# GpSimd work moved away from the routing chain, and unsplit 32-column conditioning products, in a hybrid attention and expert block

## The chip, the cores and the metric

One core of one Trainium2 chip. The metric is the device time of one execution in microseconds (us); less is better. The core has a tensor engine (PE, with its weight loads listed apart as PEld), a vector engine (DVE), a scalar engine (ACT), GpSimd (POOL), and a sync engine (SP) that here only issues transfers. Sixteen DMA engines carry all transfers.

## The reference

One layer over 512 latent tokens and 256 context tokens of width 1024. Six modulation vectors come from `silu(c) @ w_ada + b_ada` (w_ada is 1024 x 6144), for the latent vector c and for the context vector c_ctx. The tokens are normalized and modulated, projected by one matrix, and go through two attentions (grouped-query, and differential with 4 heads), which are gated, merged and projected; the result is added to x. Then comes the expert layer:

```
logits = h @ router_w + router_b;  top 4 of 32 experts per token, softmax over the 4
gate = min(xe @ w_gate[e] + b_gate[e], 7);  up = clip(xe @ w_up[e] + b_up[e], -7, 7)
act = (up + 1) * (gate * sigmoid(1.702 * gate));  y = act @ w_down[e] + b_down[e]
x = x + g_m * (sum of the token's 4 expert outputs, weighted)
```

All is float32. The 32 experts' matrices are 32 x 3 x 4 MB and are read once.

## The kernel before, in words

**Precision.** A float32 product is either made directly (the tensor engine then runs each product as two instructions, each with its own weight load), or "split": ACT rounds the weight block to fp32r (`wh`), DVE or POOL subtracts to get the rest (`wl`), and two or three faster fp32r products replace the one.

**Conditioning** (lines 181 to 314). The first two modulation vectors (`w_ada` columns 0 to 2047, two halves `hf` of 8 row blocks `k` of 512 KB each) are needed before anything can be projected. SP loads the blocks in order; even blocks go to four buffers `araw`, odd ones to two buffers `wraw` and a third spare one. After the second block SP loads the four tiles of x (512 KB each) and, after block 5, two small tables (256 KB each). Blocks 1 and 4 of a half are multiplied directly (two products of 128x512), the other six are split on ACT (L163) and DVE (L164) and take four fp32r products each. The left operand has only 4 columns (c and c_ctx, high and low parts), so the result stands in 4 partitions of `p_mod`. `columns` (L258) copies each 512-wide row out of PSUM, turns it into columns with four small transposes, and adds the bias (L267, L268); L313 finishes the scale `Ac`. Between the products the tensor engine transposes the normalized x (`channels`, 8 times 4 transposes, L227). After that the projections start.

**The middle** (lines 419 to 916) is projections, attention and their merge. The last three modulation vectors but one are summed on DVE as `acc` and `gm_bc` and spread over the partitions by `ada_end` (L679: two direct products with ones of 128x512, two ACT copies); `gm_bc` (the gate of the expert layer) is finished at L892, although it is first read by the experts.

**Output projection and routing** (lines 919 to 1104). Eight groups of products (n = 0, 1 by token tile i = 0 to 3) make x1 = x + attention. For n = 1 each tile then goes through a chain: `scaled` (L1004, two halves on POOL), `routed` (an rsqrt on DVE, L1013 makes h2, L1014 and L1015 write h2 and x1 to DRAM from POOL's queue, the last h2 from ACT's), and three stages that run later: transposes, logits (16 instructions on the tensor engine, then a string of small 128x32 operations on DVE, L1028 to L1043, that finds the top 4) and ranks (L1045). The stages of the last tiles are issued under `tc.high_priority(300)` (L1171). Then expert 0 is placed (`placed`, `gathered`: one-hot, positions, an indirect gather of its tokens from POOL's queue), the counts of all experts are sorted (L1219 to L1258), which ends in `perm` (L1246), the order in which the other 31 experts are taken. SP reads `perm` to know which weights to load next.

**The experts** (lines 1108 to 1424). Weights come in blocks of 1 MB (384 of them) into 13 places, which become free as blocks are used up. The first 12 blocks belong to expert 0 and are loaded while the routing runs; block 13 and later need `perm`. Experts alternate: a large one (128 slots, its weights split; `ahead` runs the ACT cast L1158 and the subtraction L1160 up to four half blocks in front of the tensor engine) and a small one (64 slots, direct products in two groups of 64 columns, L1284, whose places the products themselves free). The first four subtractions are on POOL, all later ones on DVE. `ahead(3)` (L1216) makes the first three half blocks ready before the sort. The two zeroed buffers `xg` for gathered tokens are set at L1167. The loop at L1408 stands under `tc.manual_schedule`: on PE, ACT and DVE its order is the written one, with small jobs hooked in ahead of a product's block k. One of them is `act_of(l + 1)`, four transposes of the small expert's activations at block 4 of the large expert's `down`.

Elsewhere a scheduler orders each engine's instructions by readiness and priority, and each engine and each transfer queue then works strictly in that order.

Of the kernel before, what the change touches and what calls it, by code (L numbers as in the profile page):

```python
# [32 lines left out]
def tile_hybrid_block(  # L33
# [169 lines left out]
    sil4 = sp.tile([128, NK, 4], FT, name="sil4")  # L203
    DVE.memset(sil4, 0.0)
    silr = sp.tile([128, NK, 4], FR, name="silr")
    for w in range(2):
        DVE.tensor_copy(sil4[:, :, 2 * w], sil[:, :, w])
        DVE.tensor_copy(silr[:, :, 2 * w], sil[:, :, w])
        DVE.tensor_sub(silr[:, :, 2 * w + 1], sil[:, :, w], silr[:, :, 2 * w])
# [45 lines left out]
    p_mc = ps.tile([128, 16, 4], FT, name="pc", bufs=1)  # L255
    md = sp.tile([128, 16, 2], FT, name="md")

    def columns(hf):  # L258

        for n in (2 * hf, 2 * hf + 1):  # L260
            row = xin[0:4, n % 2, 0:512] if hf else hraw[6 + n][0:4]
            (ACT.copy if n % 2 else DVE.tensor_copy)(row, p_mod[0:4, n])
            for j in range(4 * n, 4 * n + 4):
                PE.transpose(p_mc[:, j], row[:, (j % 4) * 128:(j % 4 + 1) * 128], ident[:4, :4])
        js = slice(8 * hf, 8 * hf + 8)
        pairs = p_mc[:, js].rearrange("p j (w a) -> p j w a", a=2)
        DVE.tensor_add(md[:, js], pairs[:, :, :, 0], col(cols[:, 24 + 8 * hf:32 + 8 * hf], 2))  # L267
        DVE.tensor_add(md[:, js], md[:, js], pairs[:, :, :, 1])  # L268

    for hf in range(2):  # L270
        for k in range(NK):
            w = w_ada[k * 128:(k + 1) * 128, hf * D:(hf + 1) * D].rearrange("p (o d) -> p o d", o=1)
            if k in (0,2,4,6):
                raw = sp.tile([128, 1, D], FT, name="araw", bufs=4)
                SP.dma_start(raw, w)
            else:
                raw = load_raw(w, 1, D)
            if k in (1,4):
                for n in range(2):
                    mm(p_mod[0:4, 2 * hf + n], sil4[:, k], raw[:, 0, n * 512:(n + 1) * 512], False, k == NK - 1)  # L280
            else:
                h, l = split_w(raw)
                for n in range(2):
                    ns = slice(n * 512, (n + 1) * 512)
                    mm(p_mod[0:4, 2 * hf + n], silr[:, k], h[:, 0, ns], k == 0, False)
                    mm(p_mod[0:4, 2 * hf + n], silr[:, k], l[:, 0, ns], False, k == NK - 1)
# [605 lines left out]
    for a, scale in ((acc[0], 0.5), (acc[1], 1.0), (gm_bc, 1.0)):  # L892
        ada_end(ps.tile([128, D], FT, name="S", bufs=2), a, scale)
# [72 lines left out]

    def expert_bias(j):
# [32 lines left out]
    def scaled(i, n):  # L1000
# [3 lines left out]
        POOL.tensor_mul(h2s[i][:, ns], x1[i][:, ns], sc_bc[:, ns])  # L1004
# [65 lines left out]
    for n in range(2):  # L1070
        ns = slice(n * 512, (n + 1) * 512)
        for i in range(4):
            p = ps.tile([128, D], FT, name=("pg", "pu")[i % 2], bufs=1)[:, ns]
            if n:
                channels_x1(i, 0)
            for k in range(NK):
# [16 lines left out]
            if n:  # L1093
                scaled(i, 0)
# [56 lines left out]
    def ahead(n=BEFORE):  # L1151

        while len(split) < n and at_split[0] < len(to_split):
# [6 lines left out]
            (DVE if at_split[0] > 3 else POOL).tensor_sub(wl, raws[i][:, a], wh)  # L1160
# [5 lines left out]
    place, xg = {}, []  # L1166
    for b, n in enumerate((D, 512)):  # L1167
        t = xp.tile([128, n], FT, name=f"xg{b}")
        POOL.memset(t, 0.0)
        xg.append(t)  # L1170
# [41 lines left out]

    placed(0, one_hot(0))
    gathered(0)
    fetch(2)
    ahead(3)  # L1216
# [36 lines left out]
    DVE.tensor_copy(rkms, srt[:, 768:896].rearrange("p (i e) -> p i e", i=4))  # L1253
    weights = srt[:, 896:1024].rearrange("p (i e) -> p i e", i=4)
    DVE.tensor_copy(auxs[:, :, :, 1], weights)
    DVE.tensor_sub(auxs[:, :, :, 2], weights, auxs[:, :, :, 1])
    for u in range(2):
        POOL.tensor_add(halvesr[:, u], blocks[:, 2 * u], blocks[:, 2 * u + 1])  # L1258
    f1.close()
# [148 lines left out]
    with tc.manual_schedule(engines={mybir.EngineType.PE, mybir.EngineType.Activation, mybir.EngineType.DVE}):  # L1408
# [7 lines left out]
        for l in range(2, E, 2):  # L1416
# [4 lines left out]
            down(l, {1: lambda: input_of(l + 2), 4: lambda: act_of(l + 1)})  # L1421
# [129 lines left out]
```

## Time and profile before

| what | value |
|---|---|
| runs shown | 1625.44, 1627.09, 1629.03 us; median 1627.09 |
| the profiled execution | 1623.81 us, span of its instructions 1621.9 us |
| PE, PEld busy | 1537.2 us (95%), 1047.6 us (65%) |
| DVE, ACT, POOL busy | 1056.4 us (65%), 754.1 us (46%), 222.0 us (14%) |
| transfers | 483.43 MB, mean 298 GB/s |

The profile shows one execution. Each engine runs its own queue; a row of the timeline gives start, duration, engine, line, operation and operands, and in brackets how long the engine stood idle before it and what released it. A stall inside an instruction is no idle time: it appears as an instruction that is far longer than others of its kind. A matmul that follows another closely is listed longer than its share, since they overlap.

### The profile page before, as it was taken

To read this page: it belongs to the slowest core of one execution; us is meant where nothing else is said; L and a number is where in the kernel's file an instruction comes from. 1 tells how busy PE (TensorE), PEld (TensorE's weight loads), DVE (VectorE), ACT (ScalarE), POOL (GpSimd) and SP (SyncE) were. 2 spreads that over 40 slices of the span, in tenths; PEclk is the share of its full clock that TensorE was granted. 3 is DMA by queue.
4 is the path that set the end of the run, shared out by engine and by line. 5 is a ranking of instruction groups with operands and counts; after the bars stand their busy time and mean duration, and the time that the engine had idled before them with its cause. 6 is when DMAs were issued, how large, how long until landed. Compare 5 with 4: busy or idle time off the path is not lost. (4 is left out here: it accounts for less than half of the span.)

```text
span 1621.9 us, 20787 instructions
## 1 busy us (share of the span) xinstructions
PE 1537.2 (95%) x7303; PEld 1047.6 (65%) x7303; DVE 1056.4 (65%) x1668; ACT 754.1 (46%) x1051; POOL 222.0 (14%) x209
## 2 busy tenths in 40 slices
PE   7999999989999689999999999999999999999997
PEld 2778877778877564666666665656666565566564
DVE  6888888756877865566566575564565655656654
ACT  5668834256633243354445344443444434434442
POOL 3431000141001520010110110100101101001000
PEclk9999999999999879999999999999999999999999
DMA  8320055411365578999999999999999999999994
GB/s 315 91 66 27 27 169 166 146 53 40 105 194 208 220 290 356 405 403 421 406 405 423 402 410 408 394 413 395 398 412 387 411 402 387 418 389 395 411 401 153
DMA packets 102430, 483.43 MB, mean 298 GB/s; under 512 B 11393, under 2 KB 33082, under 8 KB 53170
## 3 DMA queue, kind: packets, MB, share of 16 engines
q1 hardware_dynamic: 91458, 453.71, 70.8%
q0 software_dynamic: 10720, 27.82, 6.0%
q8 instruction: 60, 0.98, 0.2%
q10 hardware_dynamic: 144, 0.52, 0.1%
q14 instruction: 48, 0.39, 0.1%
HBM read 473.62 MB, written 16.78 MB: 302 GB/s over the span
## 5 line engine op out<-in xcount | busy, mean ns | idle before, releaser
L1160 DVE TENSOR_TENSOR wl<-g,wh 128x1024 fp32r<-128x1024 f32 x110 | 130.7, 1222 | 61.0 <-ACT wh L1158 52.1
L1158 ACT CAST wh<-g 128x1024 fp32r<-128x1024 f32 x110 | 110.5, 1047 | 73.9 <-DMA g<-in_w_down_dram 31.9
L1160 DVE TENSOR_TENSOR wl<-raw,wh 128x1024 fp32r<-128x1024 f32 x86 | 103.9, 1239 | 53.4 <-ACT wh L1158 46.3
L1158 ACT CAST wh<-raw 128x1024 fp32r<-128x1024 f32 x90 | 90.9, 1047 | 62.8 <-DMA raw<-in_w_down_dram 23.8
L1160 DVE TENSOR_TENSOR wl<-x,wh 128x1024 fp32r<-128x1024 f32 x70 | 83.8, 1223 | 50.3 <-ACT wh L1158 42.0
L1158 ACT CAST wh<-x 128x1024 fp32r<-128x1024 f32 x70 | 71.2, 1048 | 70.0 <-DMA x<-in_w_down_dram 34.6
L1333 POOL CAST spread<-halvesr 128x128 fp32r<-128x128 f32 x16 | 4.6, 291 | 598.2 <-PE py L60 598.2
L60 PE MATMUL pg<-wh,xH 128*128 128x512 f32 x256 | 82.3, 403 | 0.0
L60 PE MATMUL pu<-wh,xH 128*128 128x512 f32 x256 | 81.8, 401 | 0.0
L60 PE MATMUL pg<-wh,xL 128*128 128x512 f32 x256 | 80.9, 397 | 0.0
L60 PE MATMUL pg<-wl,xH 128*128 128x512 f32 x256 | 80.6, 396 | 0.0
L60 PE MATMUL pu<-wh,xL 128*128 128x512 f32 x256 | 80.5, 395 | 0.0
L60 PE MATMUL pu<-wl,xH 128*128 128x512 f32 x256 | 80.5, 395 | 0.0
L564 DVE TENSOR_REDUCE mx<-S 128x1 f32<-128x768 f32 x64 | 60.4, 953 | 30.0 <-PE S L60 29.8
L567 ACT ACTIVATE P<-S,nb,rsq 128x768 f32<-128x768 f32 x64 | 63.6, 996 | 31.5 <-DVE nb L566 31.4
L1284 PE MATMUL py<-g,xS 128*64 128x512 f32 x328 | 77.6, 598 | 0.0
L163 ACT CAST wh<-wraw 128x1024 fp32r<-128x1024 f32 x54 | 56.8, 1055 | 40.7 <-DMA wraw<-in_w_in_dram 11.4
L1160 DVE TENSOR_TENSOR wl<-acc,wh 128x1024 fp32r<-128x1024 f32 x36 | 43.2, 1223 | 28.4 <-ACT wh L1158 23.9
L1160 DVE TENSOR_TENSOR wl<-y,wh 128x1024 fp32r<-128x1024 f32 x38 | 45.4, 1222 | 21.7 <-ACT wh L1158 18.1
L164 DVE TENSOR_TENSOR wl<-wraw,wh 128x1024 fp32r<-128x1024 f32 x39 | 47.9, 1232 | 16.9 <-ACT wh L163 16.8
L1284 PE MATMUL py<-raw,xS 128*64 128x512 f32 x248 | 58.7, 597 | 0.0
L60 PEld LDWEIGHTS pg<-wl,xH 128*128 128x128 f32 x256 | 48.3, 189 | 11.8
(466 smaller groups left out, 3734.4 us busy)
## 6 DMA issues: line engine op xcount, KB each, us to landing
g<-in_w_up_dram SPq DMA_DIRECT2D x42, 1024.0 KB, 18.6
g<-in_w_down_dram SPq DMA_DIRECT2D x38, 1024.0 KB, 19.7
g<-in_w_gate_dram SPq DMA_DIRECT2D x36, 1024.0 KB, 21.2
raw<-in_w_gate_dram SPq DMA_DIRECT2D x34, 1024.0 KB, 22.7
raw<-in_w_down_dram SPq DMA_DIRECT2D x29, 1024.0 KB, 17.7
raw<-in_w_up_dram SPq DMA_DIRECT2D x27, 1024.0 KB, 21.4
wraw<-in_w_ada_dram SPq DMA_DIRECT2D x40, 512.0 KB, 4.6
x<-in_w_gate_dram SPq DMA_DIRECT2D x20, 1024.0 KB, 23.5
```

What stands on the lines that cost most here:

```text
L60: PE.matmul(o, l, r, start=start, stop=stop)
L163: ACT.copy(h, raw)
L164: (sub or DVE).tensor_sub(l, raw, h)
L564: DVE.reduce_max(mx, S, axis=AX)
L567: ACT.activation(P, S, AF.Exp, bias=nb, scale=rs, accum_out=sm)
L1158: ACT.copy(wh, raws[i][:, a])
L1160: (DVE if at_split[0] > 3 else POOL).tensor_sub(wl, raws[i][:, a], wh)
L1284: PE.matmul(p[64 * n:64 * n + 64], X[:, k], raws[i][:, a, n * 512:(n + 1) * 512], start=False, stop=True, skip_group_check=True)
L1333: POOL.tensor_copy(s[:, :, 1], halvesr[:, :, r:r + 1].to_broadcast([128, 2, SLOTS]))
```

## The change

In the conditioning no block is split: the left operand is padded to 32 columns (`sil32`), block b writes to partitions 32 (b mod 4) onward, two blocks are taken at a time, and `fold` sums the four groups while it turns rows into columns. In the routing, the split subtractions, half of the last tile's `scaled` and the zeroing of `xg` are taken from POOL or done earlier, the first `ahead(3)` moves behind the sort, and `ada_end` of `gm_bc` moves to just ahead of the placing of expert 0. In the expert loop one hook moves from block 4 to block 5.

```diff
--- before.py
+++ after.py
@@ -200,13 +200,12 @@
     DVE.tensor_scalar(s2, s2, 0.5, 0.5, op0=OP.mult, op1=OP.add)
     DVE.tensor_mul(s2, s2, cc)
 
-    sil4 = sp.tile([128, NK, 4], FT, name="sil4")
-    DVE.memset(sil4, 0.0)
-    silr = sp.tile([128, NK, 4], FR, name="silr")
-    for w in range(2):
-        DVE.tensor_copy(sil4[:, :, 2 * w], sil[:, :, w])
-        DVE.tensor_copy(silr[:, :, 2 * w], sil[:, :, w])
-        DVE.tensor_sub(silr[:, :, 2 * w + 1], sil[:, :, w], silr[:, :, 2 * w])
+    sil32 = sp.tile([128, NK, 32], FT, name="sil32")
+    DVE.memset(sil32, 0.0)
+    DVE.tensor_copy(sil32[:, :, 0:2], sil)
+
+    fold = sp.tile([128, 2], FT, name="fold")
+    DVE.reduce_sum(fold, ident.rearrange("p (j m) -> p m j", m=32)[:, 0:2], axis=AX)
 
     ms = sp.tile([128, 8], FT, name="ms")
     rr = sp.tile([128, 8], FT, name="rr")
@@ -252,38 +251,36 @@
                 POOL.tensor_mul(o2[:, :, :, a], s4[:, :, :, a], rep(g2[:, :, 1 - a], 4))
 
     p_mod = ps.tile([128, 4, 512], FT, name="pmod")
-    p_mc = ps.tile([128, 16, 4], FT, name="pc", bufs=1)
+    p_mc = ps.tile([128, 16, 2], FT, name="pc", bufs=1)
     md = sp.tile([128, 16, 2], FT, name="md")
 
     def columns(hf):
 
         for n in (2 * hf, 2 * hf + 1):
-            row = xin[0:4, n % 2, 0:512] if hf else hraw[6 + n][0:4]
-            (ACT.copy if n % 2 else DVE.tensor_copy)(row, p_mod[0:4, n])
+            row = xin[:, n % 2, 0:512] if hf else hraw[6 + n]
+            (ACT.copy if n % 2 else DVE.tensor_copy)(row, p_mod[:, n])
             for j in range(4 * n, 4 * n + 4):
-                PE.transpose(p_mc[:, j], row[:, (j % 4) * 128:(j % 4 + 1) * 128], ident[:4, :4])
+                mm(p_mc[:, j], row[:, (j % 4) * 128:(j % 4 + 1) * 128], fold, True, True)
         js = slice(8 * hf, 8 * hf + 8)
-        pairs = p_mc[:, js].rearrange("p j (w a) -> p j w a", a=2)
-        DVE.tensor_add(md[:, js], pairs[:, :, :, 0], col(cols[:, 24 + 8 * hf:32 + 8 * hf], 2))
-        DVE.tensor_add(md[:, js], md[:, js], pairs[:, :, :, 1])
+        DVE.tensor_add(md[:, js], p_mc[:, js], col(cols[:, 24 + 8 * hf:32 + 8 * hf], 2))
 
     for hf in range(2):
+        raws = []
         for k in range(NK):
             w = w_ada[k * 128:(k + 1) * 128, hf * D:(hf + 1) * D].rearrange("p (o d) -> p o d", o=1)
-            if k in (0,2,4,6):
+            if k % 2 == 0:
                 raw = sp.tile([128, 1, D], FT, name="araw", bufs=4)
                 SP.dma_start(raw, w)
             else:
                 raw = load_raw(w, 1, D)
-            if k in (1,4):
+            raws.append(raw)
+            if k % 2:
+
                 for n in range(2):
-                    mm(p_mod[0:4, 2 * hf + n], sil4[:, k], raw[:, 0, n * 512:(n + 1) * 512], False, k == NK - 1)
-            else:
-                h, l = split_w(raw)
-                for n in range(2):
-                    ns = slice(n * 512, (n + 1) * 512)
-                    mm(p_mod[0:4, 2 * hf + n], silr[:, k], h[:, 0, ns], k == 0, False)
-                    mm(p_mod[0:4, 2 * hf + n], silr[:, k], l[:, 0, ns], False, k == NK - 1)
+                    for b in (k - 1, k):
+                        rows_ = slice(32 * (b % 4), 32 * (b % 4) + 32)
+                        PE.matmul(p_mod[rows_, 2 * hf + n], sil32[:, b], raws[b][:, 0, n * 512:(n + 1) * 512],
+                                  start=b < 4, stop=b >= 4, skip_group_check=True)
             if hf == 0 and k == 1:
                 for i in range(4):
                     SP.dma_start(xin[:, i], x2[i * 128:(i + 1) * 128])
@@ -889,7 +886,7 @@
             next(fill, None)
     opened["yp"] = open_pool("yp2", "right", stack=yst)
     yBH, yBL = halves("yB", yB, DVE)
-    for a, scale in ((acc[0], 0.5), (acc[1], 1.0), (gm_bc, 1.0)):
+    for a, scale in ((acc[0], 0.5), (acc[1], 1.0)):
         ada_end(ps.tile([128, D], FT, name="S", bufs=2), a, scale)
 
 
@@ -964,6 +961,12 @@
     for g in range(4):
         DVE.tensor_copy(diag[32 * g:32 * g + 32], marks[32 * g:32 * g + 32, 0, 32 * g:32 * g + 32])
 
+    xg = []
+    for b, n in enumerate((D, 512)):
+        t = rp.tile([128, n], FT, name=f"xg{b}")
+        POOL.memset(t, 0.0)
+        xg.append(t)
+
     def expert_bias(j):
         b = braw[32 * j:32 * j + 32]
         if j == 1:
@@ -1001,7 +1004,7 @@
         if n == 0:
             h2s[i] = fp.tile([128, D], FT, name="h2", bufs=2)
         ns = slice(n * 512, (n + 1) * 512)
-        POOL.tensor_mul(h2s[i][:, ns], x1[i][:, ns], sc_bc[:, ns])
+        (DVE if i == 3 and n else POOL).tensor_mul(h2s[i][:, ns], x1[i][:, ns], sc_bc[:, ns])
 
     def routed(i):
 
@@ -1073,6 +1076,7 @@
             p = ps.tile([128, D], FT, name=("pg", "pu")[i % 2], bufs=1)[:, ns]
             if n:
                 channels_x1(i, 0)
+                scaled(i, 0)
             for k in range(NK):
                 if n and i and k == 4:
                     stages[i - 1][0]()
@@ -1091,7 +1095,6 @@
             DVE.tensor_add(x1[i][:, ns], x1[i][:, ns], t)
             ACT.activation(t, x1[i][:, ns], AF.Square, scale=1.0 / 32.0, accum_out=sqs[:, i, n:n + 1])
             if n:
-                scaled(i, 0)
                 scaled(i, 1)
                 stages.append(routed(i))
                 if i:
@@ -1157,17 +1160,13 @@
             wh = xp.tile([128, D], FR, name="wh", bufs=BEFORE + 1)
             ACT.copy(wh, raws[i][:, a])
             wl = xp.tile([128, D], FR, name="wl", bufs=BEFORE)
-            (DVE if at_split[0] > 3 else POOL).tensor_sub(wl, raws[i][:, a], wh)
+            DVE.tensor_sub(wl, raws[i][:, a], wh)
             split[i, a] = wh, wl
             at_split[0] += 1
             if a:
                 used_up(i)
 
-    place, xg = {}, []
-    for b, n in enumerate((D, 512)):
-        t = xp.tile([128, n], FT, name=f"xg{b}")
-        POOL.memset(t, 0.0)
-        xg.append(t)
+    place = {}
     with tc.high_priority(300):
         stages[3][0]()
         stages[2][2]()
@@ -1210,10 +1209,10 @@
             in_offset=bass.IndirectOffsetOnAxis(ap=place[e][0][:, 0:1], axis=0),
             bounds_check=(2 * T if small else T) - 1, oob_is_err=False)
 
+    ada_end(ps.tile([128, D], FT, name="pg", bufs=1), gm_bc, 1.0)
     placed(0, one_hot(0))
     gathered(0)
     fetch(2)
-    ahead(3)
 
 
     srt = ps.tile([128, D], FT, name="py", bufs=1)
@@ -1250,12 +1249,14 @@
     DVE.tensor_copy(bye, srt[:, 512:768].rearrange("p (a t) -> p a t", a=2))
     for a in range(2):
         mm(srt[:, 768 + 128 * a:896 + 128 * a], bye[:, a], blocks.rearrange("p g e -> p (g e)"), True, True)
-    DVE.tensor_copy(rkms, srt[:, 768:896].rearrange("p (i e) -> p i e", i=4))
-    weights = srt[:, 896:1024].rearrange("p (i e) -> p i e", i=4)
-    DVE.tensor_copy(auxs[:, :, :, 1], weights)
-    DVE.tensor_sub(auxs[:, :, :, 2], weights, auxs[:, :, :, 1])
     for u in range(2):
         POOL.tensor_add(halvesr[:, u], blocks[:, 2 * u], blocks[:, 2 * u + 1])
+    with tc.manual_schedule(engines={mybir.EngineType.Activation, mybir.EngineType.DVE}):
+        DVE.tensor_copy(rkms, srt[:, 768:896].rearrange("p (i e) -> p i e", i=4))
+        weights = srt[:, 896:1024].rearrange("p (i e) -> p i e", i=4)
+        DVE.tensor_copy(auxs[:, :, :, 1], weights)
+        DVE.tensor_sub(auxs[:, :, :, 2], weights, auxs[:, :, :, 1])
+        ahead(3)
     f1.close()
 
 
@@ -1418,7 +1419,7 @@
             gate(l + 1)
             up(l)
             up(l + 1, {5: lambda: act_of(l)})
-            down(l, {1: lambda: input_of(l + 2), 4: lambda: act_of(l + 1)})
+            down(l, {1: lambda: input_of(l + 2), 5: lambda: act_of(l + 1)})
             down(l + 1, {3: lambda: input_of(l + 3)})
     ex.close()
     right.close()
```

## Rows read from the trace of the kernel before

**Rows 1.** Windows: length; PE, PEld, DVE, ACT, POOL busy; clock; DMA share; GB/s

```profile
662.41:725.05 62.64, 62.64 (x285) 39.37 (x284) 38.44 (x40) 28.55 (x32) 6.32 (x5) 1.00 1.01 408
...
1237.01:1302.73 65.72, 63.19 (x285) 39.18 (x284) 38.35 (x40) 28.31 (x32) 6.08 (x5) 1.00 1.00 401
```

**Rows 2.** SP queue waits, 662 to 976: us total, times, longest

```profile
SPq L1144 <- PE py L1284: 72.3, 31, 6.5
```

**Rows 3.** Waits of SP's queue, 1040 to 1564

```profile
SPq L1144 <- DMA g<-in_w_gate_dram: 50.1, 21, 3.4
...
SPq L1144 <- PE py L1284: 1.7, 4, 0.6
```

**Rows 4.** A 5 us window after the first experts (columns as above)

```profile
640.00:645.00 5.00, 5.00 (x24) 2.43 (x22) 3.55 (x3) 0.00 (x0) 2.39 (x2) 1.00 0.71 249
```

**Rows 5.** Timeline of DVE in the routing

```profile
552.44 1.17 DVE L1033 TENSOR_SCALAR gt<-lg,m 128x32 f32<-128x32 f32 x1
553.54 8.94 DVE L1034 TENSOR_SCALAR eq<-lg,m 128x32 f32<-128x32 f32 x1
...
569.27 0.23 DVE L1034 TENSOR_SCALAR eq<-lg,m 128x32 f32<-128x32 f32 x1
```

**Rows 6.** Timeline of POOL in the same stretch

```profile
552.32 1.26 POOL L1004 TENSOR_TENSOR h<-x,ac 128x512 f32<-128x512 f32 x1 [0.76 <-DVE x L1091]
553.54 0.59 POOL L1015 DMA_DIRECT2D out_dram<-x  x1
554.12 1.43 POOL L1169 MEMSET xg<- 128x1024 f32 x2
555.50 6.94 POOL L1160 TENSOR_TENSOR wl<-raw,wh 128x1024 fp32r<-128x1024 f32 x3
```

**Rows 7.** Timeline, logits of tiles 2 and 3, SP after `perm`

```profile
549.48 1.87 PE L60 MATMUL py<-rws,hT 128*128 128x32 f32 x16
...
563.87 3.62 PE L60 MATMUL py<-rws,hT 128*128 128x32 f32 x16 [0.28 <-DVE rkm L1059]
...
577.32 0.36 SPq L1144 DMA_DIRECT2D x<-in_w_gate_dram  x1
```

**Rows 8.** Timeline of DVE between the sort and expert 0

```profile
579.43 0.39 DVE L1256 TENSOR_TENSOR auxs<-py,auxs 128x128 fp32r<-128x128 f32 x1
...
581.77 0.69 DVE L1319 TENSOR_TENSOR xL<-pt,xH 128x512 fp32r<-128x512 f32 x1 [1.95 <-ACT xH L1318]
```

**Rows 9.** Costliest groups of instructions: busy us, mean ns, idle before

```profile
L1160 DVE TENSOR_TENSOR wl<-raw,wh 128x1024 fp32r<-128x1024 f32 x86 | 103.9, 1239 | 53.4 <-ACT wh L1158 46.3
```

**Rows 10.** Timeline and one window of the conditioning

```profile
10.17 3.58 PE L60 MATMUL pmod<-wraw,sil 128*4 128x512 f32 x4
...
17.86 1.05 ACT L163 CAST wh<-wraw 128x1024 fp32r<-128x1024 f32 x1 [1.48 <-DMA wraw<-in_w_ada_dram]
...
22.78 1.88 PE L60 MATMUL pmod<-araw,sil 128*4 128x512 f32 x4
...
28.36 0.82 PE L227 MATMUL ptr<-marks,xin 128*128 128x128 f32 x6
...
30.00:35.00 5.00, 4.73 (x24) 1.95 (x24) 3.49 (x5) 3.63 (x6) 4.62 (x5) 1.00 0.71 250
...
39.94 0.39 PE L60 MATMUL pmod<-wl,silr 128*4 128x512 f32 x1
...
42.66 0.17 DVE L313 SCALAR_TENSOR_TENSOR Ac<-md,cols 128x16 f32<-128x16 f32 x1
```

**Rows 11.** Timeline of direct products in two 64-column groups, and after

```profile
612.50 1.94 PE L1284 MATMUL py<-raw,xS 128*64 128x512 f32 x8
...
614.36 1.03 PEld L1315 LDWEIGHTS pt<-marks,gL 128*128 128x128 f32 x8 [0.81 <-PE py L1284]
```

**Rows 12.** Timeline, first spreading product of `gm_bc`

```profile
462.51 1.02 PE L60 MATMUL S<-gm,ones_f 128*128 128x512 f32 x2
```

**Rows 13.** Waits of PE, 1200 to 1612: us in total, times, longest

```profile
PE pt L1308 <- DVE xL L1319: 10.1, 6, 1.7
```

## The prediction

> **What bounds the kernel now.** I read the kernel from its end backwards, because a stage's gain counts only if what follows passes it on. First the expert loop, by windows of one pair of experts each. An early pair takes 62.64 us with the tensor engine busy in all of it; a late one takes 65.72 us with 2.5 us of it idle; the DMA engines are busy throughout in both [rows 1]. So early pairs go at the tensor engine's pace and late ones at the pace of the transfers. The waits of SP's queue say the same: early it waits for places that products have still to free (72.3 us behind the small experts' products), late hardly ever for that (1.7 us), but for its own earlier transfers [rows 2, 3]. From the moment when all 13 places are full, the end is therefore that moment plus the time of the remaining bytes. When is that? At 640 to 645 us the transfers are idle for 29% [rows 4]: all places are full and SP waits for the tensor engine. Whatever brings expert 0 forward moves this moment, and with it the end, one for one. Nothing in the attention depends on a clock of its own, so what the conditioning gains passes through too.
>
> Second, what leads to expert 0. SP can go on only when `perm` is known, at 577.3 us [rows 7]. In front of it DVE shows two instructions that do next to nothing and last very long: a 128x32 comparison of 1.17 us and one of 8.94 us, while the same comparison for the next tile takes 0.23 us [rows 5]. POOL fills the same stretch without a gap: its half of `scaled`, a DMA issue, the zeroing of `xg` and three subtractions, until 562.4 us [rows 6]. DVE goes on right when POOL is done. So DVE is held up by POOL's work, and tile 2's masks, tile 3's logits and the sort wait behind it.
>
> Third, the conditioning. Its last product ends at 39.94 + 0.39 = 40.3 us and `Ac` comes at 42.7 us [rows 10]. The transfers are not saturated to its end (0.71 of the time, 250 GB/s, from 30 to 35 us), since buffers wait to be split.
>
> **The change part by part.** *Conditioning.* Twelve ACT casts and twelve DVE subtractions go; the 16 blocks cost 8 tensor instructions a pair. Two bounds. By transfers: block 5 lands at 17.86 us [rows 10]; ten blocks of 0.524 MB and 0.52 MB of tables are left, and at 408 GB/s [rows 1] that is 14.1 us, so the last block lands at 32.0 and its products end near 33.9 us. By the tensor engine: eight direct instructions in two column groups take 1.94 us [rows 11], while without overlap four take 1.88, and at half the clock 3.58 [rows 10]. Block 3 lands two blocks ahead of block 5, at 15.3 us. The pair of blocks 2 and 3 then runs at half the clock (3.9), six more pairs at full (6 x 1.94 = 11.6), the 32 transposes take 0.82 / 6 = 0.137 each (4.4), and eight products with `fold`, of two instructions each, bounded by two transposes each, 2.2: end at 37.4 us. Against 40.3 that is a gain of 2.9 to 6.4 us; the four `fold` products at the very end take some 0.5 us more than the four transposes did, net of one DVE addition. Between 2.4 and 5.9 I take 3.5, near the tensor engine's bound, as some transposes fit into its early gaps.
>
> *`ada_end` of `gm_bc`.* Two direct products of two instructions, the first pair listed at 1.02 us [rows 12], leave a stretch in which the tensor engine is the bound; parts of them filled waits there. Between 0 and 2.0 us of gain I take 1.0. Their new place is the routing, where the tensor engine mostly idles: 0, at worst a delay of 2.0 us if they stand ahead of a link of the chain.
>
> *POOL's work in the routing.* The stalls cost (1.17 - 0.23) + (8.94 - 0.23) = 9.65 us. What comes instead: half a `scaled` on DVE, 0.69 us like the subtraction of the same shape [rows 8]; and POOL still issues the write of x1 (0.59 us [rows 6]), behind which DVE may stand. Net 9.65 - 0.7 - 0.6 = 8.4 us. If the issue does not block and the logits of tile 3 meet the full clock (1.87 instead of 3.62 us [rows 7]), up to 2.3 us more. The earlier zeroing of `xg` and the earlier half of `scaled` lie beside tensor-bound products: 0, since nothing on DVE is last there.
>
> *`ahead(3)` behind the sort.* Its casts run on an idle ACT. Its three subtractions, at 1.24 us each [rows 9] 3.7 us, now stand on DVE between `auxs` and the first `xL`. DVE idles for 1.95 us there [rows 8], which covers that much; the first `xL`, and expert 0's second pair of products behind it, come 1.8 us later: a loss of 1.8 us, 3.7 if the cover is gone. The place of block 0 is also freed some 4 us later; DMA time is to spare until 645 us, so 0. The fourth subtraction, too, is now on DVE, within the lead of four half blocks: 0.
>
> *The hook from block 4 to 5.* In late pairs the tensor engine waits 1.7 us there, six times in 1200 to 1612 us [rows 13], and one block later it would not. But these are the pairs whose pace the transfers set: the wait moves elsewhere. 0; the upper bound is a rival below.
>
> Sum: 3.5 + 1.0 + 8.4 - 1.8 = 11.1 us. The profiled execution took 1623.8 us (1621.9 of span and 1.9 around it), so it becomes 1612.7. The median of the runs, 1627.1, stands 3.3 us above it; a median is what I forecast: 1627.1 - 11.1 = **1616 us**.
>
> **The rivals.** *Column groups take turns* (slower). Two groups of 64 overlap [rows 11]; groups of 32 are not in the trace. If a pair takes 8 x 0.47 = 3.8 us, 7.5 at half the clock, the conditioning's products end at 15.3 + 7.5 + 22.6 + 4.4 + 2.2 = 52.0 us: 12.2 us lost instead of 3.5 won, 1632 us. It is slower than before from about 3.5 us a pair. The same instruction form in the experts speaks against it.
>
> *Changing the width drains the tensor engine.* In the trace, transposes that follow 64-column products have their first weight load wait 0.81 us, yet it starts at 614.36 us, when these products end by the record (612.50 + 1.94) [rows 11]; what is lost is hardly more than that load. The Trainium skill (TensorEngine Tiling (Array Packing), Tiling Modes) says that a change of the tiling mode, not just of the tile, drains the engine. If each of some 12 changes among products, transposes and `fold` cost the whole 0.81 us, 9.7 us would go: 1626 us, no difference.
>
> *Taken back at expert 0.* Gathered tokens come as early as the sort, DVE's 1.95 us of cover is gone, and the first products, delayed, run at half the clock for 1.5 us longer: 1619.5 us. For it: the clock is at half in the routing (logits 3.62 against 1.87 us [rows 7]).
>
> *The late pairs are paced by the wait at block 4, not by transfers.* Nine pairs have the longer period (975.7 to 1564 us); if each lost just that wait, up to 1.7 us [rows 13], 15 us more would be won: 1601 us. Against it: SP's waits [rows 3].
>
> **How the numbers follow.** The forecast has 0.72, its own range being 1609 to 1621 (conditioning -1.1 to +2.4, routing -2.0 to +2.3, expert 0 -1.9). Taken back at expert 0: 0.12; groups in turn: 0.05; drained: 0.05; late pairs: 0.06. About 0.2%, 3.3 us, is what a measurement can tell from no change. Faster by more: the forecast, the late pairs and nearly all of expert 0, 0.89; within it, the drained case and a little of others, 0.07; slower, most of the groups in turn, 0.04. The range 1606 to 1624 leaves out the late pairs, the groups in turn and the drained case.
>
> **What would show it.** Right: no 128x32 operation on DVE over 2 us in the routing; SP's first transfer after `perm` some 12 us earlier; `Ac` at about 39 us; a pair's eight instructions in about 2 us; the first `xL` behind three subtractions; early pairs still 62.6 us, late ones still over 65 us with the wait gone elsewhere. Wrong: late pairs of 64 us or less; `Ac` after 43 us; DVE still long behind POOL's DMA issues; the tensor engine's start of expert 0 less than 9 us earlier.

## The result, and the profile after

The changed kernel takes 1618.12 us (median of 9 runs, 1614.49 to 1622.89), the kernel before 1627.09 (9 runs, 1623.64 to 1632.09): a ratio of 0.9943, 95% interval 0.9929 to 0.9956, 9.0 us less. A later series gave 0.9937 (0.9923 to 0.9952). The forecast was 1616, 11.1 us less, with a range of 1606 to 1624.

The two profiled executions differ by less, 1623.8 against 1619.0 us, because the one of before lies 3.3 us below its median and that of the changed kernel 0.9 us above. So I read differences stage by stage, and where they are small from several profiles. The page of the changed kernel, busy times:

```profile
PE 1540.7 (95%) x7318; PEld 1044.2 (65%) x7319; DVE 1034.0 (64%) x1655; ACT 743.1 (46%) x1039; POOL 212.2 (13%) x204
```

**The expert loop** is as it was. The windows of an early and of a late pair (columns as in [rows 1]):

```profile
658.61:721.05 62.44, 62.44 (x285) 39.43 (x284) 38.37 (x40) 28.61 (x32) 7.25 (x5) 1.00 1.02 411
...
1231.99:1297.91 65.92, 63.79 (x285) 38.87 (x284) 38.27 (x40) 28.32 (x32) 5.96 (x5) 1.00 1.01 402
```

Early pairs still go at the tensor engine's pace, late ones at the transfers'. The tensor engine's waits that the moved hook was to end, 10.1 us in [rows 13], are nearly gone, and the late pair is no shorter for it:

```profile
PE pt L1309 <- DVE xL L1320: 1.6, 6, 0.3
```

**The routing.** The timeline, lines of DVE, POOL, the queues and the tensor engine:

```profile
534.59 0.19 DVE L1032 MAX8 m<-lg 128x8 f32<-128x32 f32 x1
...
544.32 1.29 POOL L1007 TENSOR_TENSOR h<-x,ac 128x512 f32<-128x512 f32 x1 [1.58 <-DVE x L1095]
544.37 1.27 DVE L1036 TENSOR_SCALAR gt<-lg,m 128x32 f32<-128x32 f32 x1
...
553.76 0.53 POOL L1018 DMA_DIRECT2D out_dram<-x  x1 [1.82 <-DVE m L1032]
...
554.17 0.23 DVE L1036 TENSOR_SCALAR gt<-lg,m 128x32 f32<-128x32 f32 x1
554.32 0.23 DVE L1037 TENSOR_SCALAR eq<-lg,m 128x32 f32<-128x32 f32 x1
...
556.59 1.87 PE L60 MATMUL py<-rws,hT 128*128 128x32 f32 x16
...
558.87 0.34 ACTq L1017 DMA_DIRECT2D h2d<-h  x1
...
559.13 0.53 POOL L1147 DMA_DIRECT2D acc<-in_w_down_dram  x1 [4.32 <-DVE lg L1031]
...
563.75 0.16 DVE L1195 TENSOR_SCALAR ix<-pt 128x1 int32<-128x1 f32 x1 [1.09 <-PE pt L60]
...
566.30 0.19 DVE L1245 CAST perm<-py 128x32 int32<-128x32 f32 x1 [0.73 <-PE py L60]
...
568.81 1.09 POOL L1207 DMA_INDIRECT xg<-h2d,ix  x1 [9.15 <-issue]
...
574.00 1.96 PE L1316 MATMUL pt<-marks,xg 128*128 128x128 f32 x8 [5.02 <-DMA xg<-h2d,ix]
...
576.65 0.69 DVE L1320 TENSOR_TENSOR xL<-pt,xH 128x512 fp32r<-128x512 f32 x1 [2.62 <-ACT xH L1319]
...
576.72 0.88 PE L60 MATMUL pg<-wh,xH 128*128 128x512 f32 x2
```

The two comparisons of [rows 5], 1.17 and 8.94 us, take 0.23 us each (554.17, 554.32), and the logits of tile 3 now run at the full clock (1.87 us, [rows 7] had 3.62). From tile 0's first `MAX8` to `perm` the chain takes 31.7 us instead of 41.6. What is left of the mechanism is seen at 544: where POOL still multiplies for an earlier tile, DVE's small comparison ends when POOL's instruction does (1.27 beside 1.29 us).

Then 4 us are lost again. `perm` comes 9.8 us earlier than before, but the gather of expert 0 only 5.8 us (568.81 against 574.60) and its first product only 5.1 (576.72 against 581.83). The same lines of the kernel before:

```profile
534.50 0.19 DVE L1029 MAX8 m<-lg 128x8 f32<-128x32 f32 x1
...
569.01 0.35 ACTq L1014 DMA_DIRECT2D h2d<-h  x1
...
574.60 1.11 POOL L1208 DMA_INDIRECT xg<-h2d,ix  x1 [11.63 <-DVE tmp L1243]
...
576.09 0.19 DVE L1246 CAST perm<-py 128x32 int32<-128x32 f32 x1 [0.73 <-PE py L60]
576.14 0.58 POOL L1144 DMA_DIRECT2D acc<-in_w_down_dram  x1
...
581.83 1.19 PE L60 MATMUL pg<-wh,xH 128*128 128x512 f32 x2
```

`ix`, the list that the gather needs, is there at 563.75. What POOL waits for until 568.81 the profile does not name. The lines in front suggest it: the write of h2's last tile is issued at 558.87, and 0.3 us later POOL issues block 11 (`acc`, 1 MB). Before, that transfer stood behind the gather in POOL's queue (576.14). Taking the subtractions from POOL is enough to change this order: in split_on_dve (below) it leaves at 566.42 us, ahead of the gather at 573.82.

Five later profiles with the new routing list when that write landed, and in all five the gather is issued 1.1 to 1.2 us after it: the gather waits for the write. Two of the lines, from the view of transfers (the last number is us from issue to landing), of cond_ring4, where block 11 follows the write, and of block11_late, where it does not:

```profile
h2d<-h ACTq DMA_DIRECT2D x1, 512.0 KB, 9.0
...
h2d<-h ACTq DMA_DIRECT2D x1, 512.0 KB, 5.5
```

**The conditioning**, timeline and one window:

```profile
27.61 0.59 PE L282 MATMUL pmod<-araw,sil 128*32 128x512 f32 x1
...
29.06 1.95 PE L60 MATMUL pc<-fold,l 128*128 128x2 f32 x16 [0.85 <-DVE l L261]
30.94 1.06 PE L282 MATMUL pmod<-araw,sil 128*32 128x512 f32 x1
...
36.59 1.02 PE L282 MATMUL pmod<-wraw,sil 128*32 128x512 f32 x2
38.46 1.95 PE L60 MATMUL pc<-fold,xin 128*128 128x2 f32 x16 [0.85 <-DVE xin L261]
...
30.00:35.00 5.00, 5.00 (x28) 1.94 (x27) 0.17 (x1) 1.17 (x2) 0.00 (x0) 0.66 0.81 287
```

The last product ends at 36.59 + 1.02 = 37.6 us, 2.7 earlier than in [rows 10], and `Ac` comes at 40.65, 2.0 earlier. After the first columns' copies (0.85 us of waiting, then 16 narrow products) the granted clock is 0.66 for a stretch: the next products take 1.06 instead of 0.59 us.

### The profile page after: what moved, and what is told of

Same layout as the page of the kernel before. It is cut to its first block, busy times and chain, and to the rows that moved or that the text cites. A ratio compares the mean times of both kernels' runs of the same rounds, so it can differ in the third digit from the quotient of the medians.

```text
span 1617.2 us, 20753 instructions
## 1 busy us (share of the span) xinstructions
PE 1540.7 (95%) x7318; PEld 1044.2 (65%) x7319; DVE 1034.0 (64%) x1655; ACT 743.1 (46%) x1039; POOL 212.2 (13%) x204
## 5 line engine op out<-in xcount | busy, mean ns | idle before, releaser
L1163 DVE TENSOR_TENSOR wl<-raw,wh 128x1024 fp32r<-128x1024 f32 x90 | 107.8, 1229 | 60.9 <-ACT wh L1161 53.5
L163 ACT CAST wh<-wraw 128x1024 fp32r<-128x1024 f32 x48 | 50.5, 1056 | 35.7 <-DMA wraw<-in_w_in_dram 9.9
L60 PEld LDWEIGHTS pu<-wl,xH 128*128 128x128 f32 x256 | 47.8, 188 | 13.4 <-DVE wl L1163 2.0
```

Of the source, the lines that this page charges most:

```text
L60: PE.matmul(o, l, r, start=start, stop=stop)
L163: ACT.copy(h, raw)
L1163: DVE.tensor_sub(wl, raws[i][:, a], wh)
```

## The experiments

My theory after reading the traces: the stall is gone in full, the hook gives nothing, the conditioning gives its 2 us or less, and about 4 us are given back at the gather of expert 0, because block 11's transfer now shares the DMA engines with the write of h2. Rivals: the gain lies in other parts than I think; the loss at the gather was an accident of one execution, or has another cause.

What the profiles of all kernels show, in us (chain: from tile 0's `MAX8` to `perm`; write to gather: from the issue of h2's last write to that of gather 0; gather 1: the time of its instruction on POOL). The medians come from four series, and each ratio compares with the kernel before in its own series. In the first four rows the gather follows `ix` by 1.0 us, so that "write to gather" is not the write's own time there: in cond_only the write landed after 2.6 us.

| kernel | median | ratio (95%) | chain | write to gather 0 | gather 1 | `perm` to end |
|---|---|---|---|---|---|---|
| before | 1627.09 | 1 | 41.6 | 5.6 | 1.84 | 1045.8 |
| before_again | 1626.63 | 0.9995 (0.9983 to 1.0007) | 41.9 | 5.6 | 1.85 | 1047.0 |
| cond_only | 1627.24 | 1.0 (0.999 to 1.0011) | 41.9 | 5.6 | 1.84 | 1046.7 |
| split_on_dve | 1624.28 | 0.9982 (0.997 to 0.9995) | 37.3 | 7.7 | 2.99 | 1046.6 |
| routing_only | 1619.78 | 0.9956 (0.9942 to 0.997) | 30.4 | 10.1 | 1.85 | 1050.2 |
| after | 1618.12 | 0.9943 (0.9929 to 0.9956) | 31.7 | 9.9 | 4.12 | 1050.9 |
| after_again | 1617.33 | 0.9937 (0.9923 to 0.9952) | 31.8 | 9.2 | 1.85 | 1049.8 |
| hook_at_4 | 1617.28 | 0.9938 (0.9924 to 0.9953) | 31.7 | 9.9 | 1.85 | 1050.5 |
| cond_ring4 | 1615.65 | 0.994 (0.9922 to 0.9958) | 30.8 | 10.1 | 1.06 | 1048.6 |
| block11_late | 1616.67 | 0.9937 (0.9922 to 0.9953) | 31.6 | 6.6 | 1.06 | 1046.5 |
| combined | 1622.25 | 0.9962 (0.9949 to 0.9975) | 30.8 | 8.2 | 5.25 | 1054.5 |
| blocks9_11_late | 1614.34 | 0.9923 (0.9906 to 0.9941) | 30.9 | 5.6 | 4.13 | 1049.8 |
| input1_late | 1612.07 | 0.9908 (0.9891 to 0.9924) | 30.8 | 5.4 | 5.27 | 1045.1 |

### Parts of the change

**The conditioning alone** (all of the diff down to the products with `w_ada`; the routing and the experts stay as before):

```diff
-                h, l = split_w(raw)
...
+                        PE.matmul(p_mod[rows_, 2 * hf + n], sil32[:, b], raws[b][:, 0, n * 512:(n + 1) * 512],
+                                  start=b < 4, stop=b >= 4, skip_group_check=True)
```

> The kernel before with the conditioning's part of the change alone (32-column products, no splits; routing and experts as before). My theory: Ac comes 2.0 us earlier than before (42.7 to 40.7, as in the changed kernel), the attention passes that on, and the gain is 2.0 us (1.0 to 3.0; 0.12%). Rival A, the gain is used up in the attention, where clock and waits fall differently: 0 us (-0.7 to 0.7). The forecast on record said 3.5 us.

`Ac` came at 41.20 us, and the time did not move: 0.0 us, give or take 1.7. This is the rival's number, but the interval nearly reaches 2.0. More can be had from the profiles. `Ac` in the four with the old conditioning: 42.66, 42.99, 42.88, 43.15; in the five with the change's: 40.65, 41.20, 41.08, 40.95, 40.73; on average 2.0 us. At the first product of the next projection, near 219 us, the means are 219.9 and 218.3: 1.6 us. So the gain is there and most of it is passed on to 219. Behind that, executions differ by more than this among themselves, and whether it reaches the end is not settled. The rest of the change alone (next run) gains 7.2 us, the whole 9.0 and 10.2 us in its two series; that difference, too, lies within the intervals.

**The rest, without conditioning and hook:**

```diff
+        (DVE if i == 3 and n else POOL).tensor_mul(h2s[i][:, ns], x1[i][:, ns], sc_bc[:, ns])
...
+            DVE.tensor_sub(wl, raws[i][:, a], wh)
```

> The changed kernel with the old conditioning and with the hook back at block 4: POOL out of the routing, ahead(3) behind the sort and ada_end of gm_bc moved. My theory: perm comes 10 to 11 us earlier than before (gm_bc's products 1.0, the stalls 9.8), about 4 us of it are lost at the gather of expert 0, and the gain is 7 us (6 to 8; 0.43%). Rival A (the conditioning gives nothing, so this part gives all): 9 us (8.3 to 9.7). Rival B (the change in the routing is passed on in full): 10 us or more.

0.9956, 7.2 us (4.9 to 9.4): the middle of the expectation. Rival A's 9 us lies still in the interval, rival B's 10 does not. In the profile the gather comes 10.1 us behind the write, as late as in the changed kernel (9.9). This part carries most of the gain. `perm` came only 5.6 us earlier than in the first profile of before, not 10 to 11: in this execution, 2.7 us above its kernel's median, tile 0 was 5.6 us later. The chain itself is 11.2 us shorter.

**The hook back at block 4:**

```diff
-            down(l, {1: lambda: input_of(l + 2), 5: lambda: act_of(l + 1)})
+            down(l, {1: lambda: input_of(l + 2), 4: lambda: act_of(l + 1)})
```

> The changed kernel with the hook of act_of(l + 1) back at block 4. My theory (late pairs go at the transfers' pace): the same time within 1 us (1617 to 1619), the tensor engine's waits for the small experts' activations in late pairs come back (10.1 us in six waits before), and the late pairs keep their period. Rival (the hook gives what the changed kernel has over its routing part alone, 2 us): 1620 us, with late pairs longer by some 0.3 us each.

The same time as the changed kernel's (0.9938 and 0.9937 in one series). The waits are back, and cost nothing; waits of PE, 1200 to 1612 us:

```profile
PE pt L1309 <- DVE xL L1320: 10.0, 6, 1.7
```

**Is it POOL that holds DVE?** The kernel before, with the subtractions alone moved to DVE, in their old place:

```diff
-            (DVE if at_split[0] > 3 else POOL).tensor_sub(wl, raws[i][:, a], wh)
+            DVE.tensor_sub(wl, raws[i][:, a], wh)
```

> The kernel before with one change: the first four subtractions of ahead on DVE, not POOL; they stand in DVE's routing stretch, three of them ahead of the comparisons that were held (3 x 1.24 = 3.7 us). My theory (DVE is held while POOL works without a gap): POOL's stretch shrinks to a DMA issue and the zeroing of xg (2 us), the comparison of 8.94 us falls to 0.2 to 2.3 us, perm comes 8.7 - 3.7 - (0 to 2) = 3 to 5 us earlier than the same chain before, and the time falls by 2 to 5 us (1622 to 1625). Rival (the long comparison waits for something else, such as the tensor engine's logits): it stays, perm comes 3.7 us later, and the time is 1630 us.

The chain is 4.3 us shorter (37.3 us) though DVE does 3.7 us more, and the time 2.9 us (0.8 to 4.9). The timeline shows both engines:

```profile
558.22 2.07 DVE L1033 TENSOR_SCALAR gt<-lg,m 128x32 f32<-128x32 f32 x1
558.24 0.59 POOL L1015 DMA_DIRECT2D out_dram<-x  x1
...
558.43 1.89 DVE L1034 TENSOR_SCALAR eq<-lg,m 128x32 f32<-128x32 f32 x1
558.82 1.43 POOL L1169 MEMSET xg<- 128x1024 f32 x2
```

POOL's run without a gap is now an issue and the zeroing of `xg`, 558.24 to 560.25, and the comparisons that begin with it end at 560.29 and 560.32. The hold shrinks with POOL's run, so it is POOL's run that makes it; the rival would have had perm 3.7 us later.

### The 4 us behind `perm`

**The change once more, and before once more:**

> The changed kernel as it is, once more, for a second profile of it. My theory: what lies between perm and the end is a matter of the program (1050.9 us in the first profile, 1045.8 before): 1049 to 1051.5 us again, with the gather of expert 0 issued 9.5 to 10.5 us after the write of h2's last tile; what lies ahead of perm differs by up to 3 us between executions, by where the tensor engine's clock falls to half. Ratio to before 0.993 to 0.9955. Rival: the loss at the gather was an accident of one execution: perm to end under 1047 us here.

> The kernel before as it is, for a second profile of it. My theory: the first profile of before was one of its fastest executions (1623.8 against a median of 1627), because few half-clock stretches of the tensor engine fell into the 500 us ahead of the routing (1.1 us lost in it, against 1.5 to 4.9 in other profiles); a typical execution reaches perm at 577 to 581 us, and from perm to the end it is 1045 to 1047 us as in the first. Rival: perm at 576 again and the rest longer (1049 us or more), so that the changed kernel's loss behind perm would be smaller than 4 us.

The column "`perm` to end" repeats: 1045.8, 1047.0 and 1046.7 us where POOL is still busy (before, before_again, cond_only), 1050.9, 1049.8, 1050.2 and 1050.5 with the change in the routing; a loss of 3.9 us on average; cond_ring4, with the same routing, has 1048.6. It is a matter of the program. In after_again the gather left 9.2 us behind the write, a little under what was expected. The other half of the second expectation fell: `perm` came at 576.96 us, only 0.9 later, so both profiles of before are executions faster than its median.

**Block 11 behind the sort,** by an addition that reads the tile in its place:

```diff
     DVE.reduce_sum(ecol, tmp, axis=AX)
+    DVE.tensor_add(own, ecol, sh_bc[:, 0:1])
```

> The changed kernel with one tiny DVE addition (128x1) that reads sh_bc behind the sort, so that the place of block 11 is free, and its 1 MB transfer starts, only when the order of the experts is being computed. My theory: in the changed kernel this transfer starts 0.3 us after the write of h2's last tile and shares the DMA engines with it, so that the gather of expert 0 starts 9.9 us after the write is issued instead of 5.6 us as before. Here the gather starts 5.5 to 7 us after the write is issued, expert 0's first product comes 3 to 4 us earlier, and the time is 3 to 4 us below the changed kernel's, 12 to 13 us (0.76%) below before's. Rival: the gather waits for something else (the write is as slow without block 11, or POOL holds it): it still starts 9 to 10 us after the write, and the gain stays 9.0 us (8.3 to 9.7).

```profile
560.80 0.35 ACTq L1017 DMA_DIRECT2D h2d<-h  x1
...
567.39 1.10 POOL L1207 DMA_INDIRECT xg<-h2d,ix  x1 [10.63 <-DVE blocks L1240]
...
568.92 0.58 POOL L1147 DMA_DIRECT2D acc<-in_w_down_dram  x1
...
571.83 3.99 DVE L1163 TENSOR_TENSOR wl<-raw,wh 128x1024 fp32r<-128x1024 f32 x3
...
575.75 0.68 DVE L1321 TENSOR_TENSOR xL<-pt,xH 128x512 fp32r<-128x512 f32 x1
```

The gather is issued 6.6 us behind the write, and `perm` to end is 1046.5 us: in this stage the 4 us are back. The write landed after 5.5 us, against 8.9 and 9.0 in routing_only and cond_ring4. So block 11's transfer was the cause of most of the delay; the rival falls. Next in line is what the prediction had feared: the tokens are there (`xH` at 573.84), and `xL` waits for the third subtraction, until 575.75. The time does not show the gain: the median is 0.7 to 1.5 us below the changed kernel's two, not the 3 to 4 expected, and the ratio equals that of after_again. The intervals overlap, and its profile came to `perm` 1.1 to 1.9 us later than the two of the changed kernel.

**Two blocks behind the sort,** 9 and 11, with the conditioning of cond_ring4 (below):

```diff
+    DVE.tensor_add(own, ecol, sh_bc[:, 0:1])
+    DVE.tensor_add(rank, ecol, mTL[1][:, 0, 0:1].bitcast(FT))
```

> A kernel meant to be faster: the changed kernel with the conditioning's odd blocks in four places (as in cond_ring4) and with the transfers of blocks 9 and 11 both behind the sort, ahead(3) as in the changed kernel. My theory: without these two megabytes the write of h2's last tile has the DMA engines nearly to itself, the gather of expert 0 is issued within 6 us of it, right behind ix; DVE's three subtractions then stand ahead of the first or second xL (about 1.3 us, as in block11_late); gather 1 takes 1.1 to 1.9 us on POOL; perm to end 1046 to 1047 us, the time 1612 to 1614.5 us (0.991 to 0.9925). Rival (the later blocks are missed in the pairs behind): perm to end stays at 1048 us or more, 1616 us.

The write landed after 4.5 us, and the gather left 5.6 us behind its issue, 0.7 us after `ix`: block 9 had made up the rest of the delay. But the three subtractions hold the first `xL` (the two `xH` are 3.8 us apart), and gather 1 takes 4.13 us on POOL, for which the tensor engine waits 2.4 us. Gather 1 was expected at 1.1 to 1.9 us. Time 1614.34: as expected, though `perm` to end, 1049.8 us, is what the rival said.

### Gather 1, held by DVE

**A combination that lost:** block 11 late, four places, first columns at block 5, and `ahead(2)`:

```diff
-        ahead(3)
+        ahead(2)
```

> A kernel meant to be faster: the changed kernel with block 11's transfer behind the sort, the conditioning's odd blocks in four places, the first columns at block 5 of the second half and only two of ahead's subtractions ahead of the first xL (ahead(2)). My theory: gather of expert 0 within 7 us of the write; the first xL follows the first xH at once (in block11_late it came 1.3 us later, behind the third subtraction); perm to end 1044.5 to 1046 us; Ac at 38 to 39.7 us; the time 1611 to 1613.5 us (0.990 to 0.992). Rival (what is won ahead of expert 0 is given back in the early pairs): no better than block11_late, 0.9937.

Worse than the changed kernel, by 0.25%. At gather 0 the gain of block11_late did not come: the write landed after 7.1 us instead of 5.5, the gather left 8.2 us behind it (within 7 was expected) and landed after 6.4 us instead of 4.3, and the tensor engine waited 4.66 us for the tokens instead of 0.92. What slowed these transfers is not shown. `Ac` came at 40.42 us, not at 38 to 39.7. The other loss, of like size, is at gather 1:

```profile
587.18 2.34 DVE L1164 TENSOR_TENSOR wl<-cL,wh 128x1024 fp32r<-128x1024 f32 x2
587.48 5.25 POOL L1208 DMA_INDIRECT xg<-h2d,ix  x1 [11.13 <-DVE wsl L1198]
589.45 2.35 DVE L1164 TENSOR_TENSOR wl<-g,wh 128x1024 fp32r<-128x1024 f32 x2
...
592.79 2.36 DVE L1164 TENSOR_TENSOR wl<-g,wh 128x1024 fp32r<-128x1024 f32 x2 [0.99 <-ACT wh L1162]
...
598.88 0.72 PE L1311 MATMUL pt<-marks,xg 128*128 128x128 f32 x4 [3.95 <-DMA xg<-h2d,ix]
```

The gather's instruction takes 5.25 us and ends (592.73) in the gap of DVE's subtractions at 591.8 to 592.8; the tokens are 3.95 us late. In block11_late and cond_ring4 a gap of DVE of 0.3 to 0.5 us lies at its start, and it takes 1.06 us. Here DVE runs on without a gap; but it does so with `ahead(3)` as well, in the changed kernel and in blocks9_11_late (4.12 and 4.13 us), so it is not shown that `ahead(2)` made the hold. How long it is held beside subtractions varies (1.84 us in before, 4.12 in the changed kernel, both without a listed gap); what lets it in there is not shown. The Trainium skill (SBUF — State Buffer, Who interferes with whom) says that DVE and GpSimd share a port pair, and that in DVE's two-port modes whoever issues first has it for the whole instruction and the other is blocked. That DVE is blocked agrees with the hold in the routing, but that hold spans several of POOL's instructions (8.94 us beside an issue, two memsets and three subtractions). The same section of the Trainium skill reports that a `tensor_tensor` did not stall transfers issued by GpSimd, and infers the reason. This case suggests the contrary for an indirect DMA: 1.06 us in a gap, up to 5.27 beside such subtractions.

**The same with the small expert's transposes later,** so that gather 1 has time:

```diff
-        up(0, {2: lambda: hot(2), 3: lambda: input_of(1), 5: lambda: place_of(2)})
+        up(0, {2: lambda: hot(2), 5: lambda: place_of(2), 6: lambda: input_of(1)})
```

> As blocks9_11_late, with ahead(2) instead of ahead(3) and with input_of(1), the small expert's transposes, at product block 6 of up(0) instead of 3. My theory: in the combined kernel DVE lagged behind with ahead(2) and subtracted without a gap while POOL wrote gather 1's descriptors (5.25 us instead of 1.1 to 1.9), so that the tensor engine waited 4.0 us for it. Here the gather may take as long again, but it is needed some 4 us later: the wait is under 1 us, expert 0's first xL follows the first xH at once, perm to end is 1044 to 1046 us, and the time 1610.5 to 1613 us (0.990 to 0.9915). Rival (gather 1 is held as in combined and still late): a wait of 3 us or more for xg at the transposes, and 1616 us or more.

```profile
563.59 1.11 POOL L1208 DMA_INDIRECT xg<-h2d,ix  x1 [9.94 <-DVE ix L1196]
...
582.11 5.27 POOL L1208 DMA_INDIRECT xg<-h2d,ix  x1 [9.67 <-DVE wsl L1198]
...
593.94 0.63 PE L1312 MATMUL pt<-marks,xg 128*128 128x128 f32 x4
```

The gather is held as long (5.27 us), and nobody waits for it any more. 1612.07 us, 0.9908 (0.9891 to 0.9924): faster than before by 15 us and than the changed kernel by some 5. `perm` to end is 1045.1 us. One part of the expectation failed: the first `xL` (571.98) came 1.9 us behind the start of its `xH` (570.11), not at once, and cost the tensor engine 0.72 us. This kernel differs from the changed one by several edits together; what each gives in time is not separated. It is the version to keep.

### The conditioning's buffers

**Four places for the odd blocks,** in the idle ring of split halves:

```diff
-                raw = load_raw(w, 1, D)
+                raw = block("wl", 1, D, FT, 3)
+                SP.dma_start(raw, w)
```

> The changed kernel with the odd blocks of the conditioning's weights in the idle ring of split halves (4 places instead of 3, and no longer shared with the key and value weights). My theory: SP's waits for the conditioning's products (17.6 us in the changed kernel) hold back transfers that the end waits for: they fall below 8 us, the DMA share from 25 to 35 us rises from 0.76 to over 0.9, Ac comes 1 to 2 us earlier (39 to 39.7) and the time is 1 to 2 us below the changed kernel's (10 to 11 us below before's). Rival: the tensor engine's own work and its lower clock set the end of the conditioning: Ac stays at 40.4 to 40.8 and the gain at 9.0 us.

```profile
30.00:35.00 5.00, 5.00 (x31) 2.21 (x32) 0.17 (x1) 1.79 (x3) 0.00 (x0) 0.66 1.01 365
```

`Ac` came at 39.63 us, 1.0 earlier, and the DMA share from 30 to 35 us rose from 0.81 to 1.01: buffers had held back transfers (SP's waits for the conditioning's products fell from 17.6 to 8.3 us, just above the 8 expected). The clock in that stretch is 0.66 in both: the tensor engine is now the bound, as the rival had it for the whole. The time, 1615.65, is no clear gain over the changed kernel. Nor is the earlier `Ac` certain: with the same buffers it came at 39.40 in blocks9_11_late and at 40.67 in input1_late.

## Why the prediction was right, and where not

The mechanism and the result were right: faster, 9.0 us where 11.1 were forecast. That the sum came so near is in part luck: it had too little for the routing, too much for the conditioning and too small a loss at expert 0, and these errors partly cancel. The time alone does not even tell the forecast from the rival at 1619.5 us, as the interval of the ratio is 1615.5 to 1619.9 us; the traces do. (The parts' upper ends add up to 1610 us, not to the 1609 of the forecast's own range.) By its steps:

- **Stalls in the routing, 8.4 us (up to 10.7):** right, and near the upper end: the chain is 9.9 us shorter (41.6 to 31.7). Neither of the two reserves was needed: DVE does not stand behind POOL's issue at 553.76, and tile 3's logits run at the full clock.
- **Conditioning, 3.5 us:** mis-sized, 2.0 at `Ac`. The tensor-engine bound was right to 0.2 us (last product at 37.4 by the sum, 37.6 in the trace). I chose a value above the gain it gives, for transposes in early gaps, and allowed 0.5 us for the end. Instead the first columns stop the tensor engine for 0.85 us, a half-clock stretch follows, and the end takes 0.7 us more. Neither the wait nor that stretch was in the sum, so the 0.2 us are partly luck. The sum also read four products of 3.58 us in [rows 10] as half the clock, while the granted clock from 10 to 14 us is 1.00 there; why they are so long is not shown. The pair of blocks 2 and 3 was slow nevertheless (4.1 us, granted clock 0.59 from 14 to 18 us). That what the conditioning gains "passes through" is not confirmed: of 2.0 us 1.6 are left at 219 us, and none shows in the time of cond_only.
- **Column groups in turn; drains between widths:** ruled out by the traces. In cond_ring4 the last pair's eight instructions span 1.9 us (34.69 to 36.57), half of 8 x 0.47. (By the sum's own terms, groups in turn would have used up the whole gain from 3.2 us a pair, not 3.5.) In the changed kernel transposes start at 22.39 us behind products listed to 22.46 (these ends are modelled). The Trainium skill's rule of the drain (TensorEngine Tiling (Array Packing), Tiling Modes) shows no cost here at that change.
- **`ada_end`, 1.0 us:** set against the first profile of before, the stretch from DVE's last maximum over scores (`mx`, 442 us) to its copy `diag` (497 us) is shorter by 0.1 to 1.6 us in the nine profiles with the move, and between 0.8 longer and 0.5 shorter in the three without; a mean difference of 1.1. It fits, but is no larger than the spread.
- **Expert 0, -1.8 us:** the step that failed. The sum had the subtractions without cover as the loss. In fact the gather came so late that they were hidden again (`xL` waits for `xH` at 576.65), and 3.9 us were lost to the gather. The prediction weighed only block 0's place and called the transfers "to spare". It did not move POOL's own queue forward: with POOL free, block 11 left at 559.13 instead of 576.14 us and met the write that the gather waits for. The rival "taken back at expert 0" (1619.5) had the place right and the cause wrong.
- **The hook, 0:** right, shown by hook_at_4. The late pairs go at the transfers' pace.

The parts as measured, 1.6 + 1.1 + 9.9 - 3.9 = 8.7 us, make up the 9.0, as far as the uncertain first two may be added.

Of the signs of being wrong, "the tensor engine's start of expert 0 less than 9 us earlier" came true (5.1 us) and pointed to the right place. Of the signs of being right three failed: SP's first transfer after `perm` came 9.8 us earlier instead of some 12 (567.54 against 577.32), `Ac` came at 40.65 instead of 39, and the first `xL` did not wait for the subtractions.

## What to carry to other kernels

When an engine is freed, follow its transfer queue as well as its arithmetic: what it issued late by accident may now start early, beside a small transfer on the critical path. A long instruction of a trivial shape on DVE is a reason to look at POOL's line in the same microseconds, and a long DMA issue on POOL a reason to look at DVE's. Before moving work that was done ahead, see what it had kept from being late. Slack for a consumer (input_of(1) three blocks later) ended a wait here, though its producer was as slow as before.

## What was not expected of the hardware

Four column groups of 32 run at once. In the changed kernel the 16 instructions of two pairs start in fours, 0.85 us apart, and take 4.0 us in all, 30.94 to 34.97 us, most of it at half the clock (1.06 us an instruction); the pair of blocks 2 and 3 alone, two groups, took 4.1 us with instructions of the same length (14.17 to 18.25).

The tensor engine's clock can differ at the same place of the same work. Windows of 4 us where the projections begin, of the changed kernel:

```profile
216.00:220.00 4.00, 2.73 (x10) 2.08 (x10) 1.77 (x3) 1.42 (x2) 0.00 (x0) 0.84 0.64 155
220.00:224.00 4.00, 4.00 (x14) 3.15 (x13) 2.21 (x3) 1.05 (x1) 0.00 (x0) 0.74 0.90 279
```

and of the kernel before:

```profile
216.00:220.00 4.00, 2.50 (x14) 1.76 (x13) 1.98 (x3) 1.82 (x3) 0.00 (x0) 1.00 0.44 129
220.00:224.00 4.00, 4.00 (x18) 2.96 (x16) 2.42 (x2) 0.94 (x2) 0.00 (x0) 1.00 0.75 217
```

The tensor engine is about as busy in both, behind the same wait of 0.91 us for DVE, and only one falls to 1.2 GHz for some 3 us. Summed over windows of 4 us (busy time times what the granted clock lacks of 1), such stretches cost 1.1 to 6.3 us between 48 and 540 us in the thirteen profiles, which is enough to hide the conditioning's 2 us. What decides where they fall, these runs don't tell.
